# An encoder block on one core: memory rows transposed as they come, the last u tiles clear of the scan's pool, S5 outputs by one transfer a tile, attention steps between row blocks

## The chip, the core and the metric

The kernel runs on one core of one Trainium2 chip. The metric is the device time of one execution in microseconds. Three runs of the kernel before gave 1786.2, 1788.61 and 1789.65 us, so the median is 1788.61 us. A further execution was profiled; it took 1785.8 us, of which the span from its first to its last instruction is 1784.0 us.

## What is computed

The reference is one layer of a hybrid encoder block in float32, for 256 prompt tokens and 512 sample tokens (768 in all, width 1024), with 256 memory tokens for each of the two groups (512 memory rows):

```python
h = rmsnorm(x, norm_mix_g); u, q, k, v, qm, gl = split(h @ w_in)
y = S5 forward + S5 backward (64 groups of 16 channels, 64 complex states) + d * u
z = gelu(y);  s5_out = z * sigmoid(z @ s5_w_glu)
diff_out = differential attention (8 heads, two softmax maps a head, rotary, QK-norm)
mem_out  = cross-attention of qm (4 heads of 256, QK-norm) with rmsnorm(mem, mem_norm_g) @ w_mem_kv
merged = sum over the branches of sigmoid(gl + b_gate) * (branch @ w_branch)
x = x + merged @ w_out
h2 = rmsnorm(x, ffn_norm_g); x = x + (silu(h2 @ w_gate) * (h2 @ w_up)) @ w_down
```

## The kernel before

Every large product is float32 taken as three products of halves: each operand is split into a rounded part ("hi") and a rest ("lo"), and `mm3` (L754) issues hi·hi, hi·lo and lo·hi into one PSUM tile. TensorE therefore does most of the work, and the other engines prepare operands and take results out of PSUM.

**Weights.** `WStream` loads each weight tile in two halves of 512 KB (`_dma`, L533), and `_split` (L585) makes hi on ScalarE (L598) and lo either on VectorE (L604) or, where `by_dma` is set, by a copy on ScalarE (L601) and an adding transfer from GpSimd's queue (L602). Three raw halves, and four hi and four lo halves, are held at once. The order of the weights is the order of `W.add` (L695).

**Start (L956 to L1002).** The four tiles of 128 memory rows and the memory gain, broadcast to 128 partitions, are loaded ahead of the first weights. VectorE multiplies a whole row tile by the gain (L970), TensorE transposes it in eight blocks (`to_features`, L778), ScalarE makes hi (L749) and VectorE lo (L750) in steps of 512 columns. ScalarE sums the squares of the rows (L776). Then `mem_units(h)` yields units of work for head h: the products for k (four row tiles), for v (four), and for q (two feature blocks by two token segments). The k products are scaled by the row's norm `mrs` when they leave PSUM (L848). In between, the six tiles of x are normed and transposed to H.

**Memory attention.** `mem_attend` is a generator of attention steps; `Pace` draws `rate` steps for each unit of product work, here 1.2, and 1.0 beside the first two u chunks.

**S5.** `u_chunk` makes u and writes each block of 128 channels to memory in a regrouped order through a tile `ut` (`u_flush`, L279). `params` (L55 to L267) works out the S5 parameters on VectorE while chunks 2 and 3 run; `cscale` (L238) scales two sets of tables with a scratch tile for each. Chunks 2 and 3 take `ut` from a pool of two buffers. That pool and the scratch pool are then closed, and the pool for the scan (`open_work`, L283) is opened where they were. The scan runs in steps (`steps`, L453) beside the gate products "gl" (L1052 to L1067). It writes its outputs to `y_scr`.

**Differential attention and GELU.** Twelve weight tiles of q, k and v follow, six units each. At unit 6m `gelu(m-1)` computes GELU of one block of 128 channels from a tile y; three units later `gelu_load` fetches a further one. `load_y` (L447) does so by eight transfers of 16 partitions, so that partition 16g+h of y holds channel h of group g. From unit 14 on `diff_attend` draws attention steps at two thirds of a step a unit. Its `stack` (L1163) transposes q and k, and copies one half of k to the other partitions by a transfer from GpSimd's queue (L1191, tile `kst`). From unit 12 (`LOADED`) weights are split with the adding transfer.

**Third branch.** While the last v tile is worked, the memory branch's outputs are loaded over H from GpSimd's queue (L1354). `branch` (L1456) then multiplies them with `w_branch`, eight row blocks k for each product (`dense_fm`, L760), and after each product draws 1.8 attention steps for the 256-token segment or 3.6 for the 512-token one, until the attention is done.

**What sets the order.** The program text gives priorities; a planner places each instruction on its engine by its own costs when its inputs are expected, and each engine then runs its list strictly in order. Lists can therefore shift well away from an edit. SyncE's queue issues nearly all loads and stores; GpSimd's issues the adding transfers, `kst` and the reloads.

Of the kernel before, what the change touches and what calls it, by code (L numbers as in the profile page):

```python
# [23 lines left out]
class S5:  # L24
# [18 lines left out]
    def params(self, scratch, psA):  # L43
# [194 lines left out]
        def cscale(outr, outi, sr, si, ir, ii, w):  # L238
            tm = scratch.tile([128, 64, w], F32, name=f"csc{w}")
# [250 lines left out]
TILES = 6  # L490
S5_RATE = 0.76
MEM_RATE = 1.2
# [4 lines left out]
LOADED = 12  # L497
# [132 lines left out]
def hybrid_block(ctx, tc, A, outs, consts):  # L630
# [64 lines left out]
    for h in range(4):  # L695
        W.add(cols("w_mem_kv", 256 * h), 8, 256)
        W.add(cols("w_mem_kv", 1024 + 256 * h), 8, 256)
        W.add(cols("w_in", 4096 + 256 * h), 8, 256)
# [61 lines left out]
    def dense_fm(ps, w, m, x, c0, n, kk=8):  # L760
# [12 lines left out]
    def square_sum(x, pool, ss):  # L773

        jk = pool.tile([128, 1024], F32, name=uid("njk"), tag="njk", bufs=1)
        act.activation(jk, x, AF.Square, accum_out=ss)  # L776
# [53 lines left out]
    k0.tile([128, 56], F32, name="gap")  # L830
# [9 lines left out]
    def mem_units(h):  # L840

        w = W.get()
        kr = k1.tile([128, 4, 256], F32, name=uid("kr"), tag="kr")
        ss = sm.tile([128, 4], F32, name=uid("kss"), tag="kss")
        for tt in range(4):
            ps = psd("mk")
            dense_tm(ps, w, 0, 256, MT, tt)
            act.activation(kr[:, tt], ps[:, 0:256], AF.Copy, scale=mrs[:, tt : tt + 1])  # L848
            jk = k1.tile([128, 256], F32, name=uid("mjk"), tag="mjk")
            act.activation(jk, kr[:, tt], AF.Square, accum_out=ss[:, tt : tt + 1])  # L850
            yield 1.0
        w = W.get()
        mean_eps(ss, 4, 256)
        rs = rsqrt(ss, 4, "krs")
        for tt in range(4):
# [4 lines left out]
        for tt in range(4):  # L860
# [3 lines left out]
            yield 1.0  # L864
        w = W.get()
        kTh = k2.tile([128, 2, 512], F32R, name=uid("kTh"), tag="kTh", bufs=1)
# [20 lines left out]
        D[h] = (qTh, qTl), (kTh, kTl), (Vh, Vl), sqs  # L887
# [68 lines left out]
    D, P3 = {}, {}  # L956
    with tc.tile_pool(name="nrm", bufs=1) as pool, tc.tile_pool(name="nrmg", bufs=1) as pg:
        xm = [load_rows(pool, ms[0])]
        gm = bcast_load(pg, A["mem_norm_g"][0], 1024, "gmem")
        xm += [load_rows(pool, ms[tt]) for tt in range(1, 4)]  # L960
# [5 lines left out]
        xg = {}  # L966
        mss = sm.tile([128, 4], F32, name="msq", tag="kss")
        for tt in range(4):
# [3 lines left out]
            if tt == 0:  # L972
                W.ahead(0)
# [3 lines left out]
        g = bcast_load(pg, A["norm_mix_g"][0], 1024, "gmix")  # L977
        xr = [load_rows(pool, xs[tt]) for tt in range(TILES)]
        v.scalar_tensor_tensor(out=gk, in0=gk, scalar=1.0 / 16.0, in1=gq, op0=mul, op1=mul)
        units = mem_units(0)  # L980

        def norm_scales(t0, t1):

            ss = sm.tile([128, t1 - t0], F32, name=uid("xss"), tag=f"xss{t1 - t0}")
            for tt in range(t0, t1):
                square_sum(xr[tt], pool, ss[:, tt - t0 : tt - t0 + 1])
# [3 lines left out]

        rs = norm_scales(0, 2)
        for tt in range(TILES):
            next(units)
            to_features(norm_rows(pool, xr[tt], rs[tt], g), H, tt)
            if tt == 0:
                rs += norm_scales(2, TILES)
        next(units)
        next(units)
    P3["k3"] = qctx.enter_context(tc.tile_pool(name="ma3", bufs=1))
    for _ in units:  # L1000
        pass
    mat = Pace(mem_attend(), MEM_RATE)  # L1002
    for h in range(1, 4):
        for u_ in mem_units(h):
            mat.tick(u_)
# [697 lines left out]
```

## Time and profile before

| quantity | value |
| --- | --- |
| median of three runs | 1788.61 us |
| the profiled execution | 1785.8 us |
| its span | 1784.0 us |
| TensorE busy | 1762.8 us (99%) |
| VectorE busy | 1296.6 us (73%) |
| ScalarE busy | 871.6 us (49%) |
| GpSimd busy | 266.4 us (15%) |
| clock granted to TensorE, mean | 0.997 |

TensorE is called PE in the profile, its weight loads PEld, VectorE DVE, ScalarE ACT, GpSimd POOL and SyncE SP. The view by stretches gives for each stretch the busy time of each engine, the granted clock and what the DMA engines did. The chain of waits is followed back from the last instruction. In a row of the timeline the bracket is the idle time before the instruction and what ended it. A group's row has the busy time and the mean of one instruction ahead of the second bar, and the idle time behind it. Line numbers are those of the kernel before.

### The profile page before, as it was taken

Reading aid. Unit: us, or ns where it says so; the run is one execution under the profiler, and the core shown is the slowest. Engines: PE = TensorE matmul, PEld = TensorE weight load, DVE = VectorE, ACT = ScalarE, POOL = GpSimd, SP = SyncE. Lnnn points to the kernel's source line nnn. Section 1 sums busy time; section 2 is a strip of 40 time slices with the busy share of each in tenths; the row PEclk is TensorE's granted clock in tenths of the full one; section 3 lists DMA queues with packets and bytes.
Section 4 is the critical chain, followed back from the end, with each engine's and each line's share of the span. In section 5 each row is a group of like instructions: output and inputs, shape, how many; then the busy total and the mean of one; then the engine's idle time right before and its main releaser. Section 6 shows DMA issues by size and latency. Waiting matters only on the chain.

```text
span 1784.0 us, 29452 instructions
## 1 busy us (share of the span) xinstructions
PE 1762.8 (99%) x11286; PEld 1625.7 (91%) x11286; DVE 1296.6 (73%) x2385; ACT 871.6 (49%) x1842; POOL 266.4 (15%) x280
## 2 busy tenths in 40 slices
PE   8999999999999999999999999999999999999998
PEld 8999988999999998999979888888889999999997
DVE  7655748799999579778875545442699777777775
ACT  7444544777676367778765433232333333333331
POOL 0000000000000101011110101000114333333330
PEclk9999999999999999999999999999999999999999
DMA  7222656655656477454862534331312222222221
GB/s 254 72 96 95 111 137 161 150 143 133 155 143 153 126 179 191 109 113 97 177 165 83 207 127 159 116 111 54 83 48 71 71 71 72 71 71 71 72 71 71
DMA packets 194797, 207.88 MB, mean 117 GB/s; under 512 B 57824, under 2 KB 167648, under 8 KB 194656
## 3 DMA queue, kind: packets, MB, share of 16 engines
q1 hardware_dynamic: 174656, 147.27, 27.9%
q0 software_dynamic: 18848, 55.58, 14.0%
q10 hardware_dynamic: 1152, 3.15, 0.5%
q8 instruction: 89, 1.46, 0.3%
q14 instruction: 52, 0.43, 0.1%
HBM read 146.11 MB, written 32.57 MB: 100 GB/s over the span
## 4 chain that ended last, share of the span: by engine, by line
PE 92%; DVE 3%; DMA 2%; ACT 1%; issue 1%; SPq 0%; POOL 0%; DVEq 0%; ACTq 0%; POOLq 0%
PE gl L756 4%; PE gl L757 4%; PE gl L758 4%; PE br L757 3%; PE br L756 3%; PE br L758 3%; PE dn L756 3%; PE dn L757 3%; PE dn L758 3%; PE gate L756 3%; PE gate L757 3%; PE gate L758 3%; PE up L756 3%; PE up L758 3%; PE up L757 3%; PE qk L756 2%
## 5 line engine op out<-in xcount | busy, mean ns | idle before, releaser
L598 ACT ACTIVATE wh<-wr 128x1024 fp32r<-128x1024 f32 x146 | 163.7, 1122 | 104.6 <-PE br L757 27.8
L604 DVE TENSOR_TENSOR wl<-wr,wh 128x1024 fp32r<-128x1024 f32 x100 | 130.7, 1307 | 92.1 <-ACT wh L598 91.3
L756 PE MATMUL gl<-Hhi,wh 128*128 128x256 f32 (+1 forms) x384 | 132.4, 345 | 1.1 <-ACT glt L1065 1.1
L1440 DVE TENSOR_TENSOR x<-x,dn 128x512 f32<-128x512 f32 x132 | 89.0, 685 | 57.5 <-PE dn L758 57.3
L758 PE MATMUL gl<-Hhi,wl 128*128 128x256 f32 (+1 forms) x384 | 129.0, 336 | 0.0
L757 PE MATMUL gl<-Hlo,wh 128*128 128x256 f32 (+1 forms) x384 | 128.9, 336 | 0.0
L602 POOL DMA_DIRECT2D wl<-wr x46 | 40.2, 873 | 518.0 <-ACT wl L601 486.3
L756 PE MATMUL qk<-wh,Hhi 128*128 128x256 f32 x384 | 108.4, 282 | 1.6 <-ACT qksq L1131 1.6
L757 PE MATMUL qk<-wl,Hhi 128*128 128x256 f32 x384 | 108.6, 283 | 0.0
L758 PE MATMUL qk<-wh,Hlo 128*128 128x256 f32 x384 | 108.5, 283 | 0.0
L560 ACT ACTIVATE wh_S<-ws 128x512 fp32r<-128x512 f32 x70 | 41.7, 623 | 130.8 <-PE dn L758 104.1
L756 PE MATMUL dn<-wh,hidh 128*128 128x512 f32 x264 | 102.5, 390 | 1.2 <-DVE x L1440 1.0
L757 PE MATMUL dn<-wl,hidh 128*128 128x512 f32 x264 | 103.0, 390 | 0.0
L758 PE MATMUL dn<-wh,hidl 128*128 128x512 f32 x264 | 100.9, 390 | 0.0
L756 PEld LDWEIGHTS gl<-Hhi,wh 128*128 128x128 f32 x384 | 72.3, 188 | 8.3 <-ACT glt L1065 1.3
L758 PEld LDWEIGHTS gl<-Hhi,wl 128*128 128x128 f32 x384 | 72.1, 188 | 8.0
L757 PEld LDWEIGHTS gl<-Hlo,wh 128*128 128x128 f32 x384 | 72.3, 188 | 7.1
L756 PEld LDWEIGHTS qk<-wh,Hhi 128*128 128x128 f32 x384 | 73.0, 190 | 2.5 <-ACT qksq L1131 1.8
L1231 DVE TENSOR_REDUCE nm<-sc 128x1 f32<-128x512 f32 (+1 forms) x96 | 57.1, 598 | 24.7 <-PE sc L1226 23.5
L758 PEld LDWEIGHTS qk<-wh,Hlo 128*128 128x128 f32 x384 | 73.1, 190 | 0.7
L757 PEld LDWEIGHTS qk<-wl,Hhi 128*128 128x128 f32 x384 | 73.1, 190 | 0.5
L1233 ACT ACTIVATE p<-sc,nm 128x512 f32<-128x512 f32 (+1 forms) x96 | 59.0, 616 | 12.4 <-DVE nm L1231 11.9
(455 smaller groups left out, 5944.9 us busy)
## 6 DMA issues: line engine op xcount, KB each, us to landing
wr<-in_w_in_dram SPq DMA_DIRECT2D x48, 512.0 KB, 5.5
wl<-wr POOLq DMA_DIRECT2D x46, 512.0 KB, 5.1
wr<-in_w_gate_up_dram SPq DMA_DIRECT2D x44, 512.0 KB, 3.5
wr<-in_w_branch_dram SPq DMA_DIRECT2D x24, 512.0 KB, 4.2
wr<-in_w_down_dram SPq DMA_DIRECT2D x22, 512.0 KB, 3.7
glr<-gl_scr POOLq DMA_DIRECT2D x24, 384.0 KB, 3.7
wr<-in_w_mem_kv_dram SPq DMA_DIRECT2D x16, 512.0 KB, 3.4
wr<-in_w_in_dram SPq DMA_DIRECT2D x32, 256.0 KB, 4.4
```

The lines of the kernel that those rows point to most:

```text
L560: self.nc.scalar.activation(f(hi), src, AF.Copy)
L598: self.nc.scalar.activation(hi, r, AF.Copy)
L602: self.nc.gpsimd.dma_start(lo, r.bitcast(F32R), accum_op=ALU.add)
L604: self.sub.tensor_tensor(out=lo, in0=r, in1=hi.bitcast(F32), op=ALU.subtract)
L756: pe.matmul(ps, wh, xh, start=start, stop=False)
L757: pe.matmul(ps, wh, xl, start=False, stop=False)
L758: pe.matmul(ps, wl, xh, start=False, stop=stop)
L1231: v.tensor_reduce(out=nm[:, m : m + 1], in_=ps, axis=AX.X, op=ALU.max, negate=True)
L1233: act.activation(pm[:, 0:n], ps, AF.Exp, bias=nm[:, m : m + 1], accum_out=s1s[:, tt : tt + 1] if m == 0 else s2)
L1440: v.tensor_tensor(out=o, in0=o, in1=ps, op=add)
```

## The change

Four places are edited; two rates move with them.

1. **Start.** The memory gain is loaded as 8x128 and transposed by TensorE to a column. The rows are transposed unscaled as they come, two row tiles at a time, and the gain is applied as a scale for each partition when a block leaves PSUM, in steps of 256 columns instead of 512. The first weight halves are loaded between the row tiles. The squares of the rows are summed on VectorE, after the transposes. Three more dummy products are added. The k products leave PSUM unscaled, and the norm is put in later through `mrs2`, the square of `mrs`. `mem_units` is cut into `mem_k`, `mem_v` and `mem_q`, taken in the order k0 k1 v0 v1 q0 k2 q1 v2 k3 q2 v3 q3, and so are the weights. The rates go from 1.2 to 1.45 and from 1.0 to 1.5.
2. **The last u tiles.** Their pool has one buffer instead of two and lies at the other end of the memory, with a gap tile beside it, so that the scan's pool doesn't lie on it. `cscale` uses one scratch tile for both sets.
3. **S5 outputs.** y is loaded by one transfer a tile with partition 8h+g for channel h of group g, and z is written back with the same regrouping. `LOADED` goes from 12 to 24, so four halves of weights that were split with the adding transfer are split on VectorE.
4. **Third branch.** `dense_fm` can call back between row blocks; `branch` draws an eighth of a product's attention steps after each row block.

```diff
-            tm = scratch.tile([128, 64, w], F32, name=f"csc{w}")
+            tm = scratch.tile([128, 64 * 16], F32, name=f"csc{w}", tag="csc")[:, 0 : 64 * w]
+            tm = tm.rearrange("p (g w) -> p g w", w=w)
...
-        yv = y_scr.rearrange("(i h) (g k) -> g h i k", h=16, k=97)
-        for g in range(8):
-            self.nc.sync.dma_start(y[16 * g : 16 * g + 16], yv[g])
+        self.nc.sync.dma_start(y, y_scr.rearrange("(i h) (g k) -> h g i k", h=16, k=97))
...
-MEM_RATE = 1.2
+MEM_RATE = 1.45
...
-LOADED = 12
+LOADED = 24
...
+    MEM_ORDER = [("k", 0), ("k", 1), ("v", 0), ("v", 1), ("q", 0), ("k", 2), ("q", 1), ("v", 2), ("k", 3), ("q", 2),
+                 ("v", 3), ("q", 3)]
...
             mm3(ps[:, 0:n], *w(k, 128 * m, 128), xh[:, k, c0 : c0 + n], xl[:, k, c0 : c0 + n], k == 0, k == kk - 1)
+            if between and k < kk - 1:
+                between()
...
-            act.activation(kr[:, tt], ps[:, 0:256], AF.Copy, scale=mrs[:, tt : tt + 1])
+            act.activation(kr[:, tt], ps[:, 0:256], AF.Copy)
...
+        v.tensor_tensor(out=ss, in0=ss, in1=mrs2, op=mul)
         mean_eps(ss, 4, 256)
         rs = rsqrt(ss, 4, "krs")
+        v.tensor_tensor(out=rs, in0=rs, in1=mrs, op=mul)
...
+        nc.sync.dma_start(grow, A["mem_norm_g"][0].rearrange("(k p) -> k p", p=128))
+        ps = env.psa("gT")
+        pe.transpose(ps[:, 0:8], grow, env.ident[0:8, 0:8])
+        v.tensor_copy(gcol, ps[:, 0:8])
+        xm = []
+        for tt in range(2):
+            xm.append(load_rows(pool, ms[tt]))
+            W._dma()
+        xm += [load_rows(pool, ms[tt]) for tt in range(2, 4)]
...
+        for t0 in (0, 2):
+            for k0 in range(0, 8, 2):
+                ps = env.psb("nT")
+                pv = ps.rearrange("p (k t) -> p k t", k=2)
+                for k in range(2):
+                    for t in range(2):
+                        c = 128 * (k0 + k)
+                        pe.transpose(pv[:, k, 128 * t : 128 * t + 128], xm[t0 + t][:, c : c + 128], env.ident)
+                for k in range(2):
+                    sl = (slice(None), k0 + k, slice(128 * t0, 128 * t0 + 256))
+                    split_evac(MT[0][sl], MT[1][sl], pv[:, k], gcol[:, k0 + k : k0 + k + 1])
...
+            if t0 == 0:
+                for _ in range(3):
+                    pe.matmul(warm[:, 0:128], env.ident, xm[1][:, 0:128], start=True, stop=True)
+                units = mem_k(0)
+                for _ in range(2):
+                    next(units)
+        for t in range(4):
+            tc.keep_in_program_order(v.scalar_tensor_tensor(out=xm[t], in0=xm[t], scalar=1.0, in1=xm[t], op0=mul,
+                                                            op1=mul, accum_out=mss[:, t : t + 1]))
...
-            xg[tt] = pool.tile([128, 1024], F32, name=uid("nxn"), tag="nxn", bufs=2)
-            v.tensor_tensor(out=xg[tt], in0=xm[tt], in1=gm, op=mul)
-            to_features(xg[tt], MT, tt)
...
-            square_sum(xm[tt], pool, mss[:, tt : tt + 1])
...
-    mat.rate = 1.0
+    mat.rate = 1.5
...
-    up = uctx.enter_context(tc.tile_pool(name="utp2", bufs=2))
-    with tc.tile_pool(name="s5scr", bufs=1) as scr:
+    up = uctx.enter_context(tc.tile_pool(name="utp2", bufs=1, side="right"))
+    with tc.tile_pool(name="s5gap", bufs=1) as gap, tc.tile_pool(name="s5scr", bufs=1) as scr:
+        gap.tile([128, 512], F32, name="s5gap")
...
-        nc.sync.dma_start(z_scr[m], z)
+        nc.sync.dma_start(z_scr[m].rearrange("(g h) t -> h g t", h=16), z)
...
-                        dense_fm(ps, w, m, X, c0, n)
+                        between = tick and (lambda: tick((1.0 + sg) / 8))
+                        dense_fm(ps, w, m, X, c0, n, between=between)
...
-                        tick(1.0 + sg)
+                        if tick:
+                            between()
```

More of the change, by code (lines that the diff above doesn't have):

```diff
@@ L989, in norm_scales, with rest @@
             return [rs[:, t : t + 1] for t in range(t1 - t0)]
+        def rest():
+            for what, h in MEM_ORDER[1:4]:
+                yield from MEM_UNITS[what](h)
+        units = rest()
+        next(units)
         rs = norm_scales(0, 2)
+        next(units)
         for tt in range(TILES):
+            to_features(norm_rows(pool, xr[tt], rs[tt], g), H, tt)
             next(units)
-            to_features(norm_rows(pool, xr[tt], rs[tt], g), H, tt)
             if tt == 0:
                 rs += norm_scales(2, TILES)
-        next(units)
-        next(units)
+        for _ in units:
+            pass
     P3["k3"] = qctx.enter_context(tc.tile_pool(name="ma3", bufs=1))
-    for _ in units:
-        pass
     mat = Pace(mem_attend(), MEM_RATE)
-    for h in range(1, 4):
-        for u_ in mem_units(h):
-            mat.tick(u_)
-            if h == 3 and W.next == 12 and mctx is not None:
+    for what, h in MEM_ORDER[4:]:
+        for u_ in MEM_UNITS[what](h):
+            if (what, h) != ("q", 0):
+                mat.tick(u_)
+            if W.next == 12 and mctx is not None:
                 mctx.close()
```

54 lines of the change are left out of this document (31 added, 23 removed).

## The prediction

> **What bounds the kernel now.** I read the page first, for the engine that is nearest to its span, and then the view by stretches, because an engine that is busy for 99% leaves only small places where time can be won.
>
> ```profile
> span 1784.0 us, 29452 instructions
> ...
> PE 1762.8 (99%) x11286; PEld 1625.7 (91%) x11286; DVE 1296.6 (73%) x2385; ACT 871.6 (49%) x1842; POOL 266.4 (15%) x280
> ```
>
> PE is idle for 1784.0 − 1762.8 = 21.2 us in all. The work on PE hardly changes (four small instructions are added to 11286), so the change can win back only idle time, and time in which PE runs with its clock at half. The stretches say where both lie. The columns are the length, the busy time of PE, PEld, DVE, ACT and POOL with counts, the granted clock, the DMA share and GB/s.
>
> ```profile
> 10.00:20.00 10.00, 7.66 (x37) 6.67 (x37) 9.57 (x17) 8.52 (x15) 0.00 (x0) 0.67 1.06 380
> 20.00:52.00 32.00, 31.67 (x275) 31.23 (x273) 27.21 (x72) 22.72 (x46) 0.29 (x6) 1.00 0.54 182
> 52.00:300.00 248.00, 247.46 (x1701) 227.84 (x1702) 155.03 (x446) 115.90 (x220) 3.23 (x23) 1.00 0.41 103
> 300.00:312.00 12.00, 10.94 (x63) 9.45 (x62) 6.96 (x10) 5.34 (x16) 0.87 (x1) 1.00 1.00 270
> 350.00:600.00 250.00, 250.00 (x1762) 231.85 (x1762) 236.70 (x323) 171.96 (x405) 15.47 (x18) 1.00 0.57 142
> 660.00:680.00 20.00, 16.53 (x128) 16.13 (x128) 12.84 (x30) 14.37 (x28) 2.87 (x4) 0.91 0.89 210
> 890.00:922.00 32.00, 28.34 (x185) 23.69 (x183) 24.57 (x58) 20.72 (x65) 3.77 (x6) 1.00 0.52 124
> 1350.00:1784.00 434.00, 429.47 (x2251) 400.37 (x2249) 334.05 (x470) 134.27 (x234) 155.62 (x108) 1.00 0.22 70
> ```
>
> Length less PE's time is its idle time. The four edits each have a stretch: 10 to 20 us (the start) 2.34, 300 to 312 (the last u tiles and the scan's first products) 1.06, 660 to 680 (S5's outputs) 3.47, 890 to 922 (the third branch) 3.66. Two of them also lose by the clock: (1 − 0.67) · 10 = 3.3 us and (1 − 0.91) · 20 = 1.8 us. That is 15.6 us, and some 0.9 between 20 and 300. The last 434 us, idle for 4.53, aren't touched, and the 250 us from 350 on, the scan beside products, have no idle time at all: whatever the edits move, PE can't be denser there.
>
> **The change part by part.** *Start.* What ends the waits:
>
> ```profile
> 2.13 7.21 DMA nx<-in_mem_sample_dram
> ...
> 14.02 0.98 ACT memThi L749 x2
> ```
>
> ```profile
> 11.93 1.88 PE L785 MATMUL nT<-ident,nxn 128*128 128x128 f32 x12 [1.90 <-DVE memTlo L750]
> 14.07 0.80 PE L756 MATMUL mk<-wh,memThi 128*128 128x256 f32 x2 [0.27 <-ACT wh L598]
> ```
>
> ```profile
> 8.00:10.00 2.00, 1.72 (x12) 1.27 (x12) 1.85 (x3) 1.72 (x3) 0.00 (x0) 1.00 1.02 404
> ...
> 12.00:14.00 2.00, 1.81 (x12) 1.15 (x12) 2.00 (x3) 2.00 (x5) 0.00 (x0) 0.86 1.11 349
> 14.00:16.00 2.00, 1.75 (x6) 1.42 (x7) 2.00 (x6) 2.00 (x5) 0.00 (x0) 0.50 1.08 385
> ```
>
> ```profile
> L604 DVE TENSOR_TENSOR wl<-wr,wh 128x1024 fp32r<-128x1024 f32 x8 | 9.8, 1221 | 0.3 <-ACT kr L848 0.3
> L797 DVE SCALAR_TENSOR_TENSOR nxn<-nx,rqy,gmix 128x1024 f32<-128x1024 f32 x6 | 7.5, 1280 | 0.0
> L750 DVE TENSOR_TENSOR memTlo<-nT,memThi 128x512 fp32r<-128x512 f32 x8 | 5.3, 687 | 1.9 <-ACT memThi L749 1.9
> L753 DVE SCALAR_TENSOR_TENSOR Vl<-mv,mrs,Vh 128x256 fp32r<-128x256 f32 x4 | 1.8, 478 | 0.0
> L598 ACT ACTIVATE wh<-wr 128x1024 fp32r<-128x1024 f32 x8 | 8.5, 1065 | 0.8 <-PE mv L758 0.8
> L749 ACT ACTIVATE memThi<-nT 128x512 fp32r<-128x512 f32 x8 | 4.5, 599 | 1.2 <-PE nT L785 1.1
> ```
>
> In before all four row tiles stand ahead of the weights, PE transposes from DVE's scaled tiles, and the first product waits until 14.07. By then the clock is at half; it is full again after 20 us. In after the row tiles and weight halves alternate, so that four large transfers (two row tiles, two halves) have landed when four had in before, at 2.13 + 7.21 = 9.34. ACT's list has both wh ahead of the first memThi: 9.34 + 1.07 = 10.4, and a memThi of half the width takes about 0.4, so that the first product can begin near 10.8, 3.3 us earlier. From there on DVE sets the pace: its work up to the end of the stage is 16 memTlo of 256 columns (by the nearest row of that width, Vl, 16 · 0.48 = 7.7, against 8 · 0.69 = 5.5), four squares at about 1.28 = 5.1, less four gain products at about 1.28, so 2.2 us more. ACT has 16 · 0.4 = 6.4 instead of 4.5, and four squares less. I take 3.3 of earlier start, and that the clock stays up: idle time and clock lost at the start are 2.34 + 3.3 + about 0.9 (0.28 idle in 8 to 10, the rest ahead of it) = 6.5, which is the end on the good side; DVE's 2.2 and ACT's extra come off it, so −4.0. The other end, +2.7: the idle time shrinks by 0.7 only, and the clock stays at half for two steps longer (a step, in this run, is the 6.8 us at half from 13.4 to 20.3 taken as two, so 3.4, and costs 1.7).
>
> A rule of the Trainium skill speaks against this gain. Its page "TensorE: Matmul & The Clock Gate", section "Part 4: PE-mode transpose", says that transposes don't count as PE work for the clock in the way products do. By it, after's stretch of 12 transposes from about 8 us would itself bring the clock down before the products begin, and the start would give about −0.6 in place of −4.0. The 8 to 10 row, with PE at 1.72 and the clock at 1.00, is mostly transposes and doesn't agree, but the fall to half comes after the idle 10 to 12 us, so no row here tells the two apart.
>
> *Norm of k, and the order k0 k1 v0 v1 q0.* The multiplication leaves ACT's evacuation and comes back as tiny instructions on 4 columns; q0 no longer has to wait for H at 52 us (0.33 idle in 20 to 52, part of 0.54 behind it): −0.5, ends 0 and −0.9. The move of x's six norms between other units and the higher rates of attention steps I cost at nothing, since the row from 52 to 300 has DVE at 155 of 248 and ACT at 116: that cover holds as long as neither engine is a few us late for one product; if it goes, it costs up to 2.
>
> *Last u tiles.* With one buffer a tile's first copy must wait until the flush of the tile before has landed.
>
> ```profile
> 299.36 6.26 DMA u_scr<-ut
> ```
>
> ```profile
> L281 SPq DMA_DIRECT2D u_scr<-ut x4: 366/372/435, 273.8 to 299.4; - x4
> ...
> DMA to landing us min/median/max: 4.4/5.4/7.2
> ```
>
> ```profile
> 286.87 0.43 DVE L1029 COPY ut<-u 128x256 f32<-128x256 f32 x1
> ...
> 305.84 1.23 DVE L292 TENSOR_TENSOR G<-s5C,s5Ar 128x1024 f32<-128x1024 f32 x1 [5.00 <-DMA u_scr<-ut]
> ```
>
> ```profile
> 316.45 0.38 PE L325 MATMUL psK<-G,s5bpad 128*128 128x128 f32 x2
> ```
>
> ```profile
> 316.95 1.12 PE psK L325 x10
> ```
>
> Against: by the landings, one of three copies (286.87) would come 4.8 us before its buffer is free, the others by under 0.1. DVE is idle for a good third of this stretch (93 of 248), so most of these 4.8 are absorbed before the scan's tables; behind the waiting copy stand the S5 parameters on DVE. For: the scan's pool no longer lies on ut, so the chain to G doesn't wait for the last flush, 5.00 us on DVE. But PE's list in after has the first psK, which stood at 316.45, after 72 rows of the gl products, three tiles, where it had more than four, so some 4 us earlier, so the 5.00 are spent on starting the scan earlier, not on PE's idle time; the 1.06 of idle can go, and each us of wait that isn't absorbed costs one. I take +0.4; the ends are −1.1, and 4.8 − 1.1 = +3.7.
>
> *S5 outputs.* The chain ahead of the gap:
>
> ```profile
> 652.70 5.17 DMA y<-y_scr
> ...
> 659.90 2.48 DMA y<-y_scr
> ...
> 668.06 0.88 POOL wl L602
> ...
> 669.63 5.65 DMA kst<-kst
> ```
>
> ```profile
> PE sc L1225 <- DMA kst<-kst: 1.9, 1, 1.9
> PE qk L756 <- ACT qksq L1131: 1.6, 1, 1.6
> ```
>
> GpSimd issues the adding transfer (0.88) ahead of the copy kst, and PE's first scores wait 1.9 us for kst; the 3.5 us of idle then let the clock fall, 1.8 more. After has no adding transfer there, and 8 issues of y in place of 64 on SP's queue. The four halves go to DVE, 4 · 1.22 = 4.9 us of its 7.2 idle between 660 and 680, and ACT loses four copies. kst issues about 0.9 to 1.5 earlier, which doesn't cover 1.9 alone; but DVE gets y in one landing in place of the chain of two. So most goes: −4.0. The ends are −5.3 (all) and 0: one transfer of 128 partitions in pieces of 97 floats could land no earlier than eight, and DVE's 4.9 stand ahead of kst.
>
> *Third branch.* The waits between 890 and 922:
>
> ```profile
> PE br L756 <- DMA Hhi<-mo_scrh: 1.1, 1, 1.1
> PE av L1262 <- ACT aT L1250: 0.6, 2, 0.4
> ```
>
> No single wait is large. The idle 3.66 lies where PE works on attention with no products between the steps and each step waits for ACT or DVE. Drawing an eighth of the steps after each row block puts products between them; in after's order the run of attention groups without products is 15 long in place of 23, but 14 attention products in place of 22 cover the reload, whose wait can grow. −2.0, about half the idle; the ends are −3.7 and +2 (the 1.1 of the reload tripled by the eight groups that no longer cover it).
>
> Stage order beyond these, such as z written in another grouping, I put at 0, −0.5 to +2.
>
> **Sum.** −4.0 − 0.5 + 0.4 − 4.0 − 2.0 = −10.1 against the profiled 1785.8, so 1775.7. The median of the runs shown, 1788.6, stands 2.8 above that execution, and so I predict 1778.5.
>
> **The rivals.** *The clock at the start* stays at half for two steps more than forecast: 2 · 1.7 = 3.4, so 1781.9. For it: nothing holds the clock in 8 to 10.8 except transposes. Against: the products begin 3.3 us earlier and don't stop. It is also what the Trainium skill's rule gives.
>
> *Hidden edits.* PE's list stays in order and what the edits free is used up by the next late thing (the scan, dense from 350 on, speaks for it): only the two ends of clock come back, about −4, 1784.6.
>
> *Everything goes.* All idle time of the four stretches and the clock, 15.6, and 1.4 of the small waits: −17, 1771.5. Against it: attention at the third branch still waits for each step.
>
> *Slower: the one u buffer.* All three flushes land after 7.2 us, with nothing hidden but half of DVE's third of idle over the 24 us from 276 to 300: 3 · 7.2 − 4.5 = 17.1 us in the parameters' chain, less the 10.1 + 0.4 elsewhere: +6.6, 1795.2. It undoes the whole gain from 10.5 us of waiting on. Against it: two of the three copies waited for nothing in before's times, and 7.2 is the worst landing of four.
>
> *Nothing.* The change doesn't do what it says, because a planner's list shifts the waits elsewhere: 1788.6.
>
> **How the numbers follow.** Forecast 0.50, its own range 1774 to 1784; clock at the start 0.14; hidden 0.12; all idle goes 0.10; slower 0.08; nothing 0.06. A measurement of this kernel tells about 0.2%, 3.6 us, from no change, so faster means under 1785.0. Faster are the forecast, the clock case, the case where all goes, and half of the hidden one: 0.50 + 0.14 + 0.10 + 0.06 = 0.80. Same: the rest of the hidden one and nothing, 0.12. Slower 0.08. The range is 1770 (all goes, and a little) to 1790 (nothing, with the reload's +2), leaving out the u buffer's case and the good tail of the last.
>
> **What would show it.** In the changed profile: the first mk near 10.8 with PEclk at 1.00 until 52 us; copies into ut with one wait under 5 us and psK near 309 to 313; 660 to 680 with PE at 19 or more, no wait for kst over 0.5 and a clock of 1.00; 890 to 922 with PE near 30.3. Idle time of PE in all should be about 21.2 − 6 = 15, its half clock gone. It is wrong if the clock falls in a new place, if DVE waits for u_scr with PE idle behind it, or if the first attention products of the last branch wait for Hhi for over 2 us.

## The result and the profile after

The changed kernel takes 1789.88 us in the median of 17 runs (1787.03 to 1792.9), the kernel before 1786.72 us in 17 runs beside them (1784.87 to 1790.02). The ratio is 1.0017, with a 95% interval of 1.0010 to 1.0025: slower by 3.2 us, where 10.1 us less were forecast. The 1788.6 us from which the prediction counted, the median of three runs, stands 1.9 above the median of these seventeen. That 1789.88 lies just inside the stated range, which ends at 1790, is owed to that and is luck. The profiled execution took 1789.7 us, 3.9 more than that of before. From the page of after:

```profile
span 1787.8 us, 29382 instructions
...
PE 1761.9 (99%) x11293; PEld 1624.4 (91%) x11293; DVE 1301.2 (73%) x2411; ACT 861.7 (48%) x1838; POOL 261.8 (15%) x276
```

The view by stretches of after, for the stretches shown of before (length, busy time of PE, PEld, DVE, ACT and POOL with counts, granted clock, DMA share, GB/s):

```profile
10.00:20.00 10.00, 8.38 (x67) 7.81 (x68) 7.38 (x14) 6.76 (x17) 0.00 (x0) 1.00 1.04 367
20.00:52.00 32.00, 32.00 (x283) 32.00 (x282) 28.19 (x96) 24.01 (x55) 0.00 (x0) 1.00 0.52 172
52.00:300.00 248.00, 245.70 (x1674) 225.55 (x1673) 158.59 (x448) 108.20 (x209) 3.10 (x29) 1.00 0.41 102
300.00:312.00 12.00, 9.70 (x56) 8.23 (x56) 11.97 (x18) 10.44 (x27) 1.60 (x2) 1.00 1.02 242
660.00:680.00 20.00, 16.16 (x137) 15.79 (x136) 19.29 (x37) 15.04 (x34) 1.08 (x2) 1.00 0.86 205
890.00:922.00 32.00, 27.93 (x186) 24.81 (x184) 17.89 (x39) 16.30 (x49) 2.31 (x4) 0.95 0.77 171
```

In this profile only the first two stretches go as forecast: the clock stays up, and PE is idle for 1.62 us in place of 2.34, and not at all from 20 to 52. Then new idle time appears: 2.30 from 52 to 300 (0.54 before), 2.30 from 300 to 312 (1.06), 3.84 from 660 to 680 (3.47), where DVE is now busy for 19.29 of 20, and 4.07 from 890 to 922 (3.66), where the clock falls too. Two of the prediction's own signs of being wrong are among these: the clock falls in a new place, and the last branch waits for its reload (below). The first k product begins at 11.04 (timeline of PE, after):

```profile
11.04 0.38 PE L757 MATMUL mk<-wh,memThi 128*128 128x256 f32 x1 [1.04 <-ACT memThi L753]
```

PE's waits in after, from 230 to 335, from 640 to 690 and from 895 to 930 (in total, times, longest):

```profile
PE gl L757 <- ACT glt L1119: 2.3, 1, 2.3
PE u L757 <- DVE ut L1080: 1.4, 1, 1.4
```

```profile
PE qkT L1231 <- DVE qst L1241: 2.1, 1, 2.1
PE sc L1279 <- DMA kst<-kst: 1.7, 1, 1.7
```

```profile
PE br L758 <- DMA Hlo<-mo_scrl: 2.7, 1, 2.7
PE sc L1279 <- ACT p L1287: 1.4, 2, 1.2
PE br L757 <- DMA Hhi<-mo_scrh: 1.0, 1, 1.0
```

**One table for all runs.** For each profiled execution I summed, over slices of 10 us, the length less PE's busy time, and the length times what the clock lacked. The columns are the sums of both in us over four stretches, the clock's share in brackets, and the ratio to the kernel before, from the timed runs of that kernel and of before beside it. It is not the quotient of the two medians, which differs from it by up to 0.001. Outside these stretches all differ by 0.5 at most. Line numbers in what follows are those of the kernel named.

| kernel | 0–50 | 50–350 | 640–760 | 890–960 | ratio (95%) |
| --- | --- | --- | --- | --- | --- |
| before | 8.2 (3.4) | 1.9 | 5.2 (1.7) | 3.7 | |
| u_only | 6.5 | 3.5 | 7.7 (3.4) | 3.8 | 1.0011 (1.0002–1.0019) |
| s5out_only | 7.1 (1.7) | 2.3 | 5.5 (1.7) | 5.7 | 1.0005 (0.9997–1.0014) |
| loaded24_only | 5.5 | 2.0 | 3.5 | 7.5 (1.7) | 0.9997 (0.9988–1.0006) |
| shared_scratch_only | 5.3 | 2.5 | 7.4 (1.7) | 3.5 | 0.9998 (0.9989–1.0007) |
| start_only | 5.3 (1.7) | 12.1 (3.4) | 8.2 (1.7) | 7.1 (1.7) | 1.0054 (1.0041–1.0067) |
| start_shared_scratch | 3.0 | 10.4 (3.4) | 6.1 | 5.5 | 1.0036 (1.0022–1.0050) |
| after_old_s5out | 3.0 | 6.2 (1.7) | 8.1 (1.7) | 7.7 (1.7) | 1.0013 (1.0004–1.0021) |
| after | 4.1 | 4.6 | 5.1 | 7.0 (1.7) | 1.0017 (1.0010–1.0025) |
| after_no_between | 4.8 (1.7) | 7.3 (1.7) | 5.9 (1.7) | 5.5 | 1.0018 (1.0009–1.0026) |
| after_loaded12 | 4.1 | 5.2 (1.7) | 10.4 (3.4) | 7.1 (1.7) | 1.0031 (1.0019–1.0044) |
| after_old_u | 5.3 (1.7) | 14.2 (5.2) | 5.7 (1.7) | 7.5 (1.7) | 1.0037 (1.0023–1.0050) |
| after_two_u_buffers | 5.3 (1.7) | 8.5 (3.4) | 5.2 (1.7) | 4.6 | 1.0025 (1.0016–1.0034) |
| after_old_u_shared_scratch | 5.4 (1.7) | 10.2 (3.4) | 4.8 | 7.5 (1.7) | 1.0041 (1.0027–1.0054) |
| after_two_scratch | 3.8 | 4.7 (1.7) | 5.4 (1.7) | 5.2 | 1.0016 (1.0007–1.0024) |
| after_two_scratch_two_u | 5.1 (1.7) | 5.3 (1.7) | 6.9 (1.7) | 7.2 (1.7) | 1.0024 (1.0014–1.0035) |
| best_parts | 4.1 | 5.7 (1.7) | 4.1 | 9.0 (3.5) | 1.0008 (0.9999–1.0017) |

One profile is one draw: the first five kernels have the same code in the first 50 us and lost 5.3 to 8.2 there. So stages are compared by means below, and kernels by their timed runs.

### The profile page after: what moved, and what is told of

The parts are those of the page before. It is cut to its first block, busy times and chain, and to the rows that moved or that the text cites. A ratio compares the mean times of both kernels' runs of the same rounds, so it can differ in the third digit from the quotient of the medians.

```text
span 1787.8 us, 29382 instructions
## 1 busy us (share of the span) xinstructions
PE 1761.9 (99%) x11293; PEld 1624.4 (91%) x11293; DVE 1301.2 (73%) x2411; ACT 861.7 (48%) x1838; POOL 261.8 (15%) x276
## 4 chain that ended last, share of the span: by engine, by line
PE 57%; DVE 4%; DMA 2%; issue 1%; ACT 1%; POOL 0%; SPq 0%; DVEq 0%; ACTq 0%; POOLq 0%
PE br L757 4%; PE br L758 4%; PE br L759 4%; PE dn L757 3%; PE dn L758 3%; PE dn L759 3%; PE gate L757 3%; PE gate L759 3%; PE gate L758 3%; PE up L757 3%; PE up L759 3%; PE up L758 3%; PE av L1316 2%; PE qk L758 2%; PE qk L757 2%; PE qk L759 2%
## 5 line engine op out<-in xcount | busy, mean ns | idle before, releaser
L603 DVE TENSOR_TENSOR wl<-wr,wh 128x1024 fp32r<-128x1024 f32 x104 | 135.2, 1302 | 102.1 <-ACT wh L597 100.3
```

The costliest lines, as they stand in the source:

```text
L603: self.sub.tensor_tensor(out=lo, in0=r, in1=hi.bitcast(F32), op=ALU.subtract)
```

## The experiments

**The start alone.** The kernel before with edit 1, its unit order and rates; against after, the other three edits are undone.

```diff
-LOADED = 24
+LOADED = 12
...
-    up = uctx.enter_context(tc.tile_pool(name="utp2", bufs=1, side="right"))
+    up = uctx.enter_context(tc.tile_pool(name="utp2", bufs=2))
...
```

> The kernel before with the first edit alone (start, order of the memory units, their rates). Theory A, that the start gained what the traces show and the other three edits lost it: PE starts mk near 11.0 us, the clock stays at 1.00 until 52 us, the first u product comes some 3 to 6 us earlier than in before, and the time is 3.0 to 4.5 us under before, ratio 0.9975 to 0.9985. Theory B, that the start's gain is spent again by later lists whatever the other edits do (PE's list shifts, the scan waits for its tables): ratio 0.9995 to 1.0005, with the first gl product earlier but the first psY at the same time as in before.

Measured: 1799.29 us against 1787.9, ratio 1.0054, outside both theories. The start did gain: mk began at 11.16 and the first 50 us lost 5.3, though the clock fell to half for a while (0.83 from 10 to 20). The loss comes 230 us later (PE's waits from 255 to 330 of start_only):

```profile
PE b L104 <- DMA s_c_re_raw<-in_s_c_re_dram: 7.3, 1, 7.3
```

The first load of the S5 parameters is issued at 262.51 us, where before issues it at 196.85 (timeline of SP's queue, start_only and then before):

```profile
262.51 0.73 SPq L75 DMA_DIRECT2D s_lam_re_raw<-in_s_lam_re_dram  x1
```

```profile
196.85 0.73 SPq L75 DMA_DIRECT2D s_lam_re_raw<-in_s_lam_re_dram  x1
```

In before it waits for the last v product of the memory; here it waits for the last u product of chunk 1. The edit holds a second `kr` tile, 4 KB a partition, and the parameters' pool now lies on memory that is in use until then. That the second `kr` tile is the cause is inferred from this placement; that more room cures it is shown below.

**The u tiles undone in after.**

```diff
-            tm = scratch.tile([128, 64 * 16], F32, name=f"csc{w}", tag="csc")[:, 0 : 64 * w]
+            tm = scratch.tile([128, 64, w], F32, name=f"csc{w}")
-    up = uctx.enter_context(tc.tile_pool(name="utp2", bufs=1, side="right"))
-    with tc.tile_pool(name="s5gap", bufs=1) as gap, tc.tile_pool(name="s5scr", bufs=1) as scr:
-        gap.tile([128, 512], F32, name="s5gap")
+    up = uctx.enter_context(tc.tile_pool(name="utp2", bufs=2))
+    with tc.tile_pool(name="s5scr", bufs=1) as scr:
```

> After, with the last u tiles in two buffers below the scan's pool, and two scratch tiles, as before. Theory A, that the one buffer costs (PE waits 1.4 for DVE's copy at 289, and 2.3 against 1.1 for ScalarE at 306): both go back, and the time falls by 2 to 2.6 against after (ratio to before 1.0002 to 1.0008). Theory B, that the scan's earlier tables win back as much as the buffer costs: the first psK moves from 309.8 to about 313 to 316, and the time stays within 1 us of after (1.0012 to 1.0023).

Measured: 1796.01 us, ratio 1.0037, outside both ranges. The same wait, 8.0 us for s_c_re_raw, and 14.2 us lost from 50 to 350. So edit 2 isn't a gain of its own: it pays for the memory that edit 1 takes.

**LOADED 12 in after.**

```diff
-LOADED = 24
+LOADED = 12
```

> After, with four halves split by the adding transfer again (LOADED 12 as before), the new transfers of y kept. Theory A, that DVE, 19.3 of 20 us busy between 660 and 680, is what PE waits for there (qst 2.1 us, the late half of kst 1.7, the late evacuation 2.4): DVE's busy time between 640 and 680 falls by about 4.9, PE's long gaps there from 5.6 to under 3, the time by 2 to 4 against after (ratio to before 0.9995 to 1.0008). Theory B, that the order of the queues matters and DVE does not: GpSimd's adding transfer stands ahead of kst again, PE waits for kst by 1.9 or more, and the time is that of after or above (1.0015 to 1.003).

Measured: 1795.23 us, ratio 1.0031, so theory B's side and beyond it. PE's waits from 608 to 899:

```profile
PE qk L757 <- ACT qksq L1185: 2.7, 1, 2.7
PE qkT L1231 <- DVE qst L1241: 1.8, 1, 1.8
PE sc L1279 <- DVE rqt L739: 1.7, 1, 1.7
```

The stage loses 10.4. DVE has less to do, but the waits go to other steps of the same chain. It looks as if LOADED 24 is what makes y by one transfer bearable, but this is one profile, and the interval of its ratio (1.0019 to 1.0044) overlaps that of after.

**No drawing between row blocks.**

```diff
-                        between = tick and (lambda: tick((1.0 + sg) / 8))
-                        dense_fm(ps, w, m, X, c0, n, between=between)
+                        dense_fm(ps, w, m, X, c0, n)
...
-                        if tick:
-                            between()
+                        if tick:
+                            tick(1.0 + sg)
```

> After, with the third branch's attention steps drawn after each product again, and no callback between row blocks. Theory A, that drawing between row blocks is what costs: the gaps between 893 and 998 fall from 8.9 to about 6.4, the clock stays at 1.00 there, and the time falls by 3 to 4 (ratio to before 0.9995 to 1.0005). Theory B, that the late second reload of H (landing 908.0 in after, 901.2 in before) is what costs, whatever is drawn between the blocks: PE still waits 2 us or more for Hlo, attention then runs in a block of its own, and the time stays or rises by up to 2 (1.0015 to 1.003).

Measured: 1791.63 us, ratio 1.0018, that of after and in theory B's range. The instruction lists of all five engines agree with those of after from the first entry to the last, by operation, tile name and shape, but for two small VectorE records near 270 us, which start within 0.03 us of each other and stand in swapped order. So edit 4 did nothing, and the shorter run of attention groups that I credited to it belongs to another edit (see LOADED below). This run also shows what after's own code can do in another execution: its first 50 us lose 1.7 by the clock, where after lost nothing.

**Two u buffers in after.**

```diff
-    up = uctx.enter_context(tc.tile_pool(name="utp2", bufs=1, side="right"))
+    up = uctx.enter_context(tc.tile_pool(name="utp2", bufs=2, side="right"))
```

> After, with two buffers for the last u tiles, at the place that the change gave them. Theory A, that the single buffer costs PE time (1.4 to 2.0 us for the copy into ut in three profiles of the same list, and DVE's and ScalarE's work behind it): PE does not wait for a copy into ut between 280 and 300, and the time falls by 2 to 4 against after, ratio to before 0.9995 to 1.0008. Theory B, that the wait moves on to the scan's tables: PE waits 2 us or more longer for glt or psK between 300 and 320, ratio 1.0012 to 1.0025.

Measured: 1792.21 us, ratio 1.0025: theory B. No wait for ut is left, and PE waits for the scan instead (230 to 335):

```profile
PE psK L326 <- ACT R L377: 3.0, 1, 3.0
PE gl L757 <- ACT glt L1119: 1.2, 1, 1.2
```

**The second edit alone, on before** (as in the diff of the change, `cscale` and the pools).

> The kernel before with the second edit alone (one u buffer clear of the scan's pool, one scratch tile). Theory A, that one buffer costs 1.5 to 3 us wherever it stands: ratio 1.0005 to 1.0018, with PE waiting for a copy into ut. Theory B, that the edit's worth depends on the memory: without the first edit's second kr tile the parameter loads are issued near 197 us in any case, the chain to the scan's tables is freed of the flush (5.0 us on DVE), PE's 1.1 us wait for glt goes and the ratio is 0.9985 to 1.0.

Measured: 1789.9 us, ratio 1.0011: theory A's range, but not its place. No copy into ut holds up PE; it waits 2.7 us for glt in two pieces.

**The third edit alone, on before** (`load_y`, the store of z and LOADED 24).

> The kernel before with the third edit alone (y by one transfer, z regrouped, four more halves split on DVE). The prediction: 3 to 5 us less, ratio 0.997 to 0.9985, no wait for kst and the clock at 1.00 between 660 and 680. Theory A, from the trace of after, that DVE, now 19 of 20 us busy there, takes the place of kst: ratio 1.001 to 1.003, with PE waiting for qst and for evacuations.

Measured: 1787.95 us, ratio 1.0005, between the two ranges. PE's waits from 610 to 700, and one from 885 to 935:

```profile
PE qkT L1175 <- DVE qst L1185: 2.0, 1, 2.0
...
PE sc L1223 <- DMA kst<-kst: 0.5, 1, 0.5
```

```profile
PE br L755 <- DMA Hlo<-mo_scrl: 2.8, 1, 2.8
```

kst falls to 0.5, as predicted, and DVE's qst takes its place; and the reload in the third branch, whose Hlo cost 0.4 in before, costs 2.8.

**The third edit undone in after** (`load_y`, z and LOADED 12 as in before).

> After, with the third edit undone (y by eight transfers, z as before, LOADED 12). Theory A, that the third edit loses 2 to 3 us in after as its trace has it: the time falls by 2 to 3, ratio to before 0.9995 to 1.0008. Theory B, that the stage loses whatever its edit is, since all engines stand at another point of their lists when it comes (with the start alone the lists from the scan on are those of before, and it yet lost 3.8 us from the first qk to the last v): the time stays or rises by up to 4, ratio 1.0015 to 1.004.

Measured: 1790.48 us, ratio 1.0013 (1.0004 to 1.0021), between the two ranges, and not to be told from after. The stage itself lost 8.1 against 5.1.

**The start with the shared scratch, u buffers as before.** `cscale` is that of after; LOADED, `load_y`, z and `branch` are those of before.

```diff
-    up = uctx.enter_context(tc.tile_pool(name="utp2", bufs=1, side="right"))
-    with tc.tile_pool(name="s5gap", bufs=1) as gap, tc.tile_pool(name="s5scr", bufs=1) as scr:
+    up = uctx.enter_context(tc.tile_pool(name="utp2", bufs=2))
+    with tc.tile_pool(name="s5scr", bufs=1) as scr:
```

> The first edit together with the shared scratch tile of the second, and nothing else: the last u tiles keep two buffers under the scan's pool. Theory A, that the start is worth 2 to 3 us, and lost 10 us when alone only because its second kr tile pushed the S5 parameters' memory onto tiles that live until the second u chunk is flushed (loads issued at 262 us instead of 197): the loads come near 190, PE does not wait for s_c, there is no wait for a copy into ut, and the ratio is 0.9980 to 0.9993. Theory B, that an earlier start is used up at the u tiles and the scan whatever the buffers: PE waits 3 us or more longer than in before between 230 and 335, ratio 0.9995 to 1.0015.

Measured: 1792.82 us, ratio 1.0036, beyond both ranges. The smaller scratch does cure the loads (they wait for the v product again, and no wait for s_c is left). But the scan opens late (waits, 230 to 340):

```profile
PE gl L759 <- ACT glt L1119: 6.0, 1, 6.0
```

glt stands on ScalarE behind tables that wait for the last flush of ut, as in before; DVE's first G waits 9.9 us for it, where it waited 5.0 in before.

**After with the old u buffers but the shared scratch** (the same pools, the rest as in after).

> After, with the last u tiles in two buffers at their old place, but one scratch tile kept. Theory A, that of the second edit only the shared scratch is of use and the single buffer costs 3 to 4: the time falls by 3 to 5 against after, ratio to before 0.999 to 1.0005. Theory B as in the run beside it: ratio 1.001 to 1.0025.

Measured: 1794.72 us, ratio 1.0041, and a wait of 5.9 us for glt: theory A is wrong here as well.

**LOADED 24 alone, on before.**

```diff
-LOADED = 12
+LOADED = 24
```

> The kernel before with LOADED 24 alone: no adding transfer ahead of kst, y by eight transfers as before. With the kernel before (eight transfers, 12), the third edit alone (one transfer, 24) and after with 12 (one transfer, 12) it makes a square. Theory A, that the adding transfer ahead of kst is what costs in before and the y transfers are hidden: PE's idle time and lost clock between 640 and 760 fall by 2 against runs of before's list (7.0 in the mean of four), ratio 0.9985 to 0.9995. Theory B, that DVE then becomes the bound and the y transfers are what let it start earlier: idle time and lost clock stay at 7 or more, ratio 1.0005 to 1.002.

Measured: 1786.44 us, ratio 0.9997 (0.9988 to 1.0006): no difference that can be told, and between the two ranges. Its stage has the least loss of all, 3.5, with kst at 1.1. Its list has 16 attention products and transposes more before the last v product, like every kernel with the third edit or a part of it; so the shorter run in the third branch comes with this constant as well as with y's transfers.

**Which part of edit 2 costs.** Three kernels for what was still open, and one of the parts that looked best: after with two scratch tiles (the `cscale` lines of before), after with two scratch tiles and two u buffers, before with the shared scratch alone, and after with both and with `load_y`, z and `branch` as in before.

> After, with two scratch tiles for the two sets of tables again, and nothing else changed (one u buffer, gap and place as in after). Theory A, that the shared scratch is what spends the start's gain: it makes DVE finish s5bb only after s5F (at 295 and 298 us in after, at 287 and 290 in before), ScalarE's fill of s5bpad waits for it, and behind that fill stand the last copy into ut and glt, for which PE waits: s5bb is done by about 290, PE's idle time and lost clock from 300 to 350 fall under 1, and the time falls by 1.5 to 3 against after, ratio to before 0.9998 to 1.0008. Theory B, that the single u buffer does it: the time stays within 1 us of after, ratio 1.0012 to 1.0023.

> After, with two scratch tiles and two u buffers at the place of after. Theory A and B together have both costs gone: PE waits neither for a copy into ut nor for glt, idle time and lost clock from 230 to 350 fall to about 1.5 (6 to 8 in the runs of after's list), the start's 2 to 3 us stay, and the ratio is 0.9985 to 0.9998. If the start's gain is bound to be lost at the scan's tables whatever stands there, the ratio is 1.001 or more, with PE waiting for psK or glt by 2 us or more.

> The kernel before with the shared scratch tile alone. Theory A: s5bb is done at about 298 to 301 us instead of 290, ScalarE's fill and the last copy into ut come later, PE waits for glt by 2.5 us or more (1.1 in before), and the ratio is 1.0008 to 1.002, that of the second edit alone (1.0011). Theory B: the buffers are what cost, and the ratio is 0.9995 to 1.0005.

> The parts that looked best: the start, two scratch tiles, two u buffers at the place of after, LOADED 24, y by eight transfers and z as before, no callback between row blocks. If the parts add: 2 to 3 less from the start, 0.6 less from LOADED 24 alone (0.9997), ratio 0.998 to 0.9992. If the stage of the S5 outputs goes by where the engines happen to stand when it comes, 0.9995 to 1.001.

Measured: 1790.1 (1.0016), 1791.29 (1.0024), 1786.84 (0.9998) and 1789.04 us (1.0008). With two scratch tiles s5bb is done 11 us earlier, as expected (timeline of DVE, after and then after_two_scratch):

```profile
297.79 1.23 DVE L242 TENSOR_TENSOR s5bb<-s5bb,csc 128x1024 f32<-128x1024 f32 x1
```

```profile
286.83 1.22 DVE L241 TENSOR_TENSOR s5bb<-s5bb,csc 128x1024 f32<-128x1024 f32 x1
```

The wait for glt goes, PE's wait for ut rises from 1.4 to 2.1, and the timed runs don't move: theory B's range. The shared scratch alone has theory B's ratio too, though PE's wait for glt rises from 1.1 to 1.8; and the best parts together come out as the second of their two cases, with no gain. With both cured, PE waits where the first table ends (timelines of PE and DVE, and DVE's busy time by stretches, after_two_scratch_two_u):

```profile
306.83 3.83 PE L325 MATMUL psK<-G,s5bpad 128*128 128x128 f32 x16 [2.65 <-issue]
```

```profile
305.95 1.27 DVE L297 TENSOR_TENSOR G<-G,ptG 128x512 f32<-128x512 f32 x2
```

```profile
250.00:270.00 20.00, 20.00 (x113) 17.01 (x113) 10.77 (x33) 6.62 (x8) 0.48 (x2) 1.00 0.56 145
270.00:290.00 20.00, 20.00 (x126) 17.89 (x125) 19.53 (x82) 8.68 (x20) 0.98 (x6) 1.00 0.47 79
290.00:310.00 20.00, 17.36 (x91) 14.82 (x90) 19.71 (x34) 11.34 (x25) 2.23 (x5) 0.93 0.72 179
```

DVE is busy for 39.2 of the 40 us from 270 to 310, and the scan's first product begins while DVE finishes the first tables. The other two kernels with two u buffers at this place, after_two_u_buffers and best_parts, wait 3.0 us at the same products. PE comes here 1 to 2 us earlier than with the old start (first gl product at 294.8 to 295.8 in these three, 295.9 to 297.8 in the five with the old start) and has psK after 48 gl products in place of 102. In before 18.7 us lie between the first gl product and the first psK, 1.1 of them a wait; here 11.0, with a wait of 2.7: some 9 us less work. So it meets a bound that the change doesn't move. No run kept psK at its old place in PE's list, so how much of the wait that place alone makes is not shown.

## Why the prediction was wrong

**Start (−4.0).** The earlier products held: mk at 11.04 (10.8 forecast). The clock did not. After shows no half clock up to 52 us, but after_no_between, which runs the same lists, does (stretch from 10 to 20):

```profile
10.00:20.00 10.00, 8.41 (x53) 7.64 (x52) 6.04 (x12) 5.50 (x11) 0.00 (x0) 0.83 1.05 364
```

Six of the twelve profiles with the new start have 0.83 there, and two of the five with the old one have 0.67 and 0.83. In the mean of the first 50 us the old start loses 5.5 by idle time and 1.0 by the clock (6.5 in all, not before's 8.2), the new one 3.6 and 0.9 (4.4). So the start is worth −2.1, nearly all of it idle time. I took 3.3 us of half clock as the old start's own, and it was one draw.

**Order of units and H wait (−0.5).** Held: no idle time from 20 to 52, and none from 50 to 60 in all twelve profiles with the new start, where the five with the old one have 0.4 to 0.5.

**Last u tiles (+0.4, ends −1.1 and +3.7).** This is one of the two steps that failed most. The reasoning "the 5.00 are spent on starting the scan earlier, not on PE's idle time" was right in its place: psK came at 309.8. But I put the list's new place of psK at no cost. From 50 to 350 after lost 4.6 us in its profile; after, after_no_between, after_loaded12 and after_old_s5out have one list of products from the u tiles to the scan and lost 5.8 in the mean, against 2.1 for the three kernels with neither start nor edit 2 (before, s5out_only, loaded24_only): +3.7, the end of my range. The stretch holds the 0.4 to 0.5 of the H wait as well, so the u tiles and the scan cost about 4.2. Two waits make it, the one for ut (1.4) and the one for glt (2.3). Each can be cured alone, as the runs showed, and PE then waits for the next; behind them stands DVE, dense from 270 to 310. The start's gain is spent here: all twelve kernels with the new start lose 4.6 to 14.2 in this stretch, the five with the old one 1.9 to 3.5.

**S5 outputs (−4.0).** The reason held for kst (1.9 in before, 0.5 in s5out_only, though 1.7 in after), and I named DVE's 4.9 us ahead of kst as a possible cost, then put it at too little: qst, on DVE, now holds PE for 2.1. In the mean the stage loses 7.1 us in the six kernels with the old form and 5.6 in the eight with the new: −1.6. Here too the base was a draw: before's own 5.2 is the lowest of its six. The square of four forms (old y and 12: 7.1; old y and 24: 3.8, two kernels; new y and 12: 10.4, one; new y and 24: 5.6) suggests that LOADED gains and y by one transfer loses. That the y transfer loses rests on three profiles in two of the cells, and the regrouped store of z, which goes with it in every run, was not tried apart.

**Third branch (−2.0).** This step failed by most. "Drawing an eighth of the steps after each row block puts products between them" was wrong: the list is the same without it. The shorter attention run that I counted comes with the third edit. The cost came at the place that I had named as the bad end, the reload, but not by that mechanism. These are the first products that need the last Hlo, and the issue of that reload with its landing, in before and then in after (timeline of PE, and the view by tile of Hlo):

```profile
901.26 0.50 PE L757 MATMUL br<-Hlo,wh 128*128 128x512 f32 x1 [0.41 <-DMA Hlo<-mo_scrl]
...
L1354 POOL DMA_DIRECT2D Hlo<-mo_scrl x1: 873/873/873, 891.0 to 891.0; - x1
...
DMA to landing us min/median/max: 10.2/10.2/10.2
```

```profile
908.16 0.47 PE L758 MATMUL br<-Hlo,wh 128*128 128x512 f32 x1 [2.65 <-DMA Hlo<-mo_scrl]
...
L1409 POOL DMA_DIRECT2D Hlo<-mo_scrl x1: 873/873/873, 895.1 to 895.1; - x1
...
DMA to landing us min/median/max: 13.0/13.0/13.0
```

The last v product starts at 889.65 and 893.71. So the reload is issued 1.3 to 1.4 us behind it in both, and PE reaches the product that needs it 11.2 us behind it in before and 11.8 in after: the work that covers the reload has not shrunk. The reload itself takes 2.8 us longer to land. It takes 10.1 to 10.4 us in the three kernels with the old list and the old start, 12.0 to 12.4 in the three with the old list and the new start, and 12.3 to 13.5 in the eleven with the new list. In the new list a kst copy and both halves of the next weights are issued within 5.3 us of the last v product, where in the old one the second half comes at 7.0; that this is what slows the reload is not shown, and it doesn't explain the 12 us with the old list and the new start, where the issues stand as in before. Why they take longer is open.

The stretch from 890 to 960 loses 5.2 in the mean of the six kernels with the old list and 6.7 in the eleven with the new: +1.5. This mean mixes the starts. With the old start, the old list loses 3.5 to 3.8 and the new one 5.7 and 7.5 (two kernels); with the new start, both lose 6.7 in the mean (three and nine kernels). So either of the two brings the loss, they don't add, and from before to after it is +3.1.

**The sum.** Over all kernels, −2.1 + 3.7 − 1.6 + 1.5 = +1.5. The added products of the start take about 0.8 (seven records in the trace, not the four that I counted: six are 0.11 us apart, ahead of mk, and fill time that else were idle), and the slower pace of the products, below, about 0.9. That makes 3.2, as measured, but in part by luck. Where each stretch compares only kernels like before with kernels like after in start and form, it is −2.1 + 3.7 − 1.2 + 3.1 = +3.5, and 5.2 with the same two terms; the interval of the measured ratio is 1.8 to 4.5. Two of the profiles behind these means, those of after_no_between and after_old_s5out, are of executions 1.6 and 2.8 us slower than the median of their kernel. So the parts account for the result to within about 2 us.

**The rivals.** The slower one had the right place, but not the right mechanism: PE's wait for the single u buffer is 1.4 us, and two buffers alone didn't make the kernel faster (1.0025). It also took 10.5 us of waiting as needed to undo the gain: the start and the S5 outputs together gained under 4, so a loss of about 4 undid it. "Hidden edits" was the right idea for edit 1. The clock rival didn't happen in after's profile, and happened with half its price in six of the other eleven with the new start: 1.7 us lost, one step and not two. The rule of the Trainium skill ("TensorE: Matmul & The Clock Gate", "Part 4: PE-mode transpose"), by which the start would have been worth −0.6, is not decided by this: the same twelve transposes and dummy products, then 1.0 and 0.6 us of idle time, were followed by a clock that stayed up in one profile (1.00 in after) and by one that fell to half in another (0.83 in after_no_between). The measured −2.1 lies between the two.

What was not done: a kernel that has the start and an earlier chain of S5 parameters, or psK at its old place in the list. None of the versions run is measurably faster than before.

## What to carry to other kernels

Where one engine is busy for 99% and works its list in order, winning time early can just bring it sooner to the next thing that doesn't move: before an early gain is counted, find the next place where another engine is dense and the busy one takes its result. A change that takes memory in one stage can move loads in a stage far behind; look at when the later stage's loads are issued. And a term of 3 us can't be based on one profile when the same code loses between 5.3 and 8.2: several profiles of unrelated edits serve as repeats of the untouched stages.

## What the runs showed of the hardware that was not expected

**The half clock is a draw.** Two rows of the same stretch and the same start code, from u_only and then from s5out_only:

```profile
10.00:20.00 10.00, 7.40 (x56) 6.56 (x57) 9.51 (x17) 8.20 (x15) 0.00 (x0) 1.00 1.05 376
```

```profile
10.00:20.00 10.00, 8.07 (x55) 7.48 (x54) 9.60 (x15) 8.85 (x16) 0.00 (x0) 0.83 1.07 382
```

With the same code the clock lacked 0, 1.7 or 3.4 us (0.67 in before, 0.83, and 1.00 in three of five). Over all runs the loss came in pieces of about 1.7 us (half of 3.4), mostly after one idle stretch of 2 to 3 us, at the new start after 1.0 and 0.6, and with the same list now it came and now it didn't. The Trainium skill ("TensorE: Matmul & The Clock Gate", "Part 1: The HAM clock gate") speaks of a free-running window of about 3.4 us; the pieces agree with it.

**Products have two paces.** Starts of 44 steps of 128x256 products in before, and then of 8 after a group of transposes (timeline of PE):

```profile
648.91 0.28 PE L756 MATMUL qk<-wh,Hhi 128*128 128x256 f32 x1
...
653.90 0.28 PE L758 MATMUL qk<-wh,Hlo 128*128 128x256 f32 x1
...
655.12 0.28 PE L758 MATMUL qk<-wh,Hlo 128*128 128x256 f32 x1
...
656.07 0.28 PE L757 MATMUL qk<-wl,Hhi 128*128 128x256 f32 x1
```

4.99 us for 44 steps is 113 ns a product, 0.95 for 8 is 119, at a clock of 1.00. The pace changes at some interleaved groups and stays until a later one. The median spacing of the qk products was 114 ns in before and 117 in after. Summed over all products of 256, 384 and 512 columns, as the excess over the quick pace, six profiles with the old S5 list have 24.7 us in the mean and eight with the third edit 25.6: the 0.9 above. Its cause is open.
